# Five blocks of scan output turned by transposing DMAs instead of TensorE, in a hybrid decoder layer

## The chip, the cores and the metric

The kernel runs on one core of a Trainium2 chip. It has five engines with a queue each: TensorE (PE in the profile; its weight loads are PEld), VectorE (DVE), ScalarE (ACT), GpSimd (POOL) and SyncE (SP). The last three also issue DMAs; a DMA that stands in an engine's queue is issued in that queue's order (ACTq, POOLq, SPq). The metric is the device time of one execution in microseconds. The kernel before took 2245.72 us, the median of three runs between 2244.68 and 2250.13.

## The reference

One decoder layer over 2048 tokens of width 1024, with 16 learned meta tokens put in front and dropped at the end. From the normalised input one projection gives everything two branches need. One branch is a state space scan (SSD, Mamba-2) with 16 heads in four groups, behind a short convolution; the other is gated linear attention (GLA) with four heads. Both are normalised, gated and merged:

```python
u = rmsnorm(hres, norm_w)
proj = jnp.einsum('bld,dn->bln', u, w_in)
z, xbc, dt_raw, q, k, v, g_gla, a_lr, merge_g = split_cols(proj, IN_WIDTHS)
xbc = jax.nn.silu(causal_depthwise_conv(xbc, conv_w, conv_b))
...
y = y.reshape(b, l, D_SSD) * jax.nn.silu(z)
y_ssd = rmsnorm(y.reshape(b, l, SSD_GROUPS, D_SSD // SSD_GROUPS), ...)
...
gate_logit = jnp.einsum('blr,rk->blk', a_lr, gla_gate_w2) + gla_gate_b
log_a = jax.nn.log_sigmoid(gate_logit) / GLA_GATE_TEMP
...
y_gla = o.reshape(b, l, GLA_DV) * jax.nn.silu(g_gla)
branches = jnp.stack([y_ssd, y_gla], axis=2)
branch_proj = jnp.einsum('blnc,ncd->blnd', branches, w_branch)
gates = jax.nn.sigmoid(merge_g.reshape(b, l, N_BRANCH, D_MODEL))
merged = jnp.sum(gates * branch_proj, axis=2)
return hres + jnp.einsum('bld,de->ble', merged, w_out)
```

Everything is float32. On TensorE a float32 product is made of three products of operands that are split into a high and a low part.

## The kernel before

The tokens are worked in four blocks of 512; the first block (number 0 in the code) also carries the 16 meta tokens (`m0`). Each block is cut into four chunks of 128 tokens.

The first part of the kernel (to about 1480 us) makes, block by block, the projections and the two scans. A block's projections are a row of *pieces* (`proj_zm`, `proj_conv`, `proj_qk`, `proj_v`, `gla_gates`), and after every piece `step` moves each running side work one step on. The side works are Python generators: `ssd_scan` for each of four groups (started every sixth piece), `gla_scan` for each of four heads, `gates` for the decay of GLA, `fetch_u` for the next block's normalised input. A `yield` in one of them is the border of a step, so a `yield` more puts what follows behind the matmuls of one more piece. TensorE and SyncE keep exactly the order in which the code is written; ScalarE, VectorE and GpSimd are ordered by the tile scheduler, which `tc.issue_after` can bind.

A scan unit (one group or one head of one block) leaves its output as tokens by channels (`yt`, `ot`, 128 tokens x 4 chunks x 256 channels). The second part of the kernel (to the end) needs it as channels by tokens. So every unit ends with eight transposes of 128x128 on TensorE into two PSUM banks (L735 in `ssd_scan`, L974 in `gla_scan`). In `ssd_scan` ScalarE takes them out with the norm weight as scale (L737) into tiles `gg`; in `gla_scan` VectorE multiplies them into the gate tiles `gs`, also named `gg` (L975). Two DMAs on ScalarE's queue store the halves to `y` in memory (L738, L978). GLA units also use a pair of tiles `atp` (a ring of two) for the split attention matrix: ScalarE rounds the high part (L263), VectorE subtracts for the low part (L264), and TensorE multiplies (L214 to L216, in `accum`).

Other places that the change touches: `fetch_u` stores each of the eight tiles of the normalised input (`u_left`, L346) from ScalarE's queue; `load_w` splits weights into a high part on ScalarE (L175) and a low part on GpSimd (L177, tiles `whl`); `gates` makes the decay of the GLA heads in two pairs (products L488 with PSUM banks `pj` and `pt` in the first block, evictions L490 on VectorE and L491 on ScalarE, sums L500); `gla_scan` adds the state of the meta tokens (L881, L882); `make_sums` adds up weights for the second part on GpSimd (L83, stores L86 on ScalarE's queue).

The second part multiplies gates, branches and the output in a scheme of seven products instead of eight (`stages`, sums of weights in `load_a` and `sum_a`). At its end `out_stage` adds the residual (L1250), squares (L1251), takes the root on GpSimd (L1261, L1276), scales (L1283, L1285, L1287) and stores (L1377 on ScalarE's queue, L1432 on SyncE's).

Of the kernel before, what the change touches and what calls it, by code (L numbers as in the profile page):

```python
# [9 lines left out]
F32R = mybir.dt.float32r  # L10
BF16 = mybir.dt.bfloat16
# [4 lines left out]
P = 128  # L16
# [3 lines left out]
BLK = 512  # L20
# [23 lines left out]
def trunk_kernel(ctx: ExitStack, tc: tile.TileContext, xm, xmt, w_feat, w_tok, w_v3, w_zm, w_br, w_o,  # L44
# [225 lines left out]
    def load_u(b):  # L270
# [66 lines left out]
        for kt in range(KT):  # L337
# [8 lines left out]
            nc.scalar.dma_start(u_left[b][kt], xk[:, m0:])  # L346
# [121 lines left out]
    def gates(o):  # L468
# [12 lines left out]
        for h2 in range(0, GH, 2):  # L481
# [14 lines left out]
            for h in (h2, h2 + 1):  # L496
                def sums(h=h):
                    nc.vector.tensor_tensor(gmt[:, h % 2, :tt], gmt[:, h % 2, :tt], g_all[:, h, :tt], op=ALU.subtract)
                    for a, n in chunks:
                        nc.vector.tensor_tensor_scan(g_all[:, h, a:a + n], ones[:, :n], gmt[:, h % 2, a:a + n], 0.0,  # L500
                                                     op0=ALU.mult, op1=ALU.add)
# [81 lines left out]
    def proj_conv(o, g):  # L583
        tt = o.tt
        feats = o.feats[g] = []
        for j in range(4):
# [9 lines left out]
            nc.gpsimd.tensor_copy(tails[:, ti, :], cin[:, tt:tt + 3])  # L596
# [9 lines left out]
    cbs, evicted, convd = {}, [], []  # L606
# [5 lines left out]
    def fetch_cb(o, g, c):  # L612
        cbs[g, c] = cb = mk(spool, [P, 4, P], F32, "cb", bufs=3)
        nc.sync.dma_start(cb, o.cumd[4 * g:4 * g + 4, c * P:(c + 1) * P].unsqueeze(0).to_broadcast([P, 4, P]))

    def ssd_scan(o, g):
# [64 lines left out]
        def after(c):  # L681
# [10 lines left out]
            nc.gpsimd.tensor_tensor(sv, sv, hb(dec[:, ci, hs], P), op=ALU.mult)  # L692
# [36 lines left out]
        yield  # L729
        if not m0 and not g:  # L730
            yield
# [54 lines left out]
    def gla_scan(o, h, last=False):  # L786
# [92 lines left out]
        if m0:  # L879
            ps = bank(pc, "pc")  # L880
# [85 lines left out]
        for c in range(NCH):  # L966
            nc.scalar.activation(ot[:, c], ot[:, c], AF.Identity, scale=r[:, c:c + 1])
        yield
# [256 lines left out]
    def out_stage():  # L1225
        fns, res, ssq, at_once = [], {}, {}, []
# [10 lines left out]
        def use(n, i, t, ps, snap, cols=None):  # L1237
# [13 lines left out]
            nc.scalar.activation(jk[:, c], r[:, c], AF.Square, accum_out=q[:, k:k + 1])  # L1251
            row = n, i, t
            if row == at_once[-1] or (first and (n, i) in [w[:2] for w in at_once[1:]]):
# [4 lines left out]
                if k == 2:  # L1258
                    last = nc.vector.scalar_tensor_tensor(q[:, 0:1], q[:, 2:3], 1.0 / D, q[:, 0:1],
# [5 lines left out]
            elif row in at_once:  # L1265
                scale(*row)
                finish(*row)
# [69 lines left out]
    def load_sum_a(st, n):  # L1337
        st.load_a(n)
        st.sum_a(n)
# [91 lines left out]
    for dst, src in stores:  # L1431
        nc.sync.dma_start(dst, src)  # L1432
# [88 lines left out]
```

## Time and profile before

| | before |
|---|---|
| runs, median (lowest, highest) | 2245.72 us (2244.68, 2250.13) |
| profiled execution | 2246.09 us, span 2244.0 us |
| mean granted TensorE clock | 0.999 |
| TensorE busy | 2213.1 us (99%) |
| VectorE busy | 1574.2 us (70%) |
| ScalarE busy | 1188.8 us (53%) |
| GpSimd busy | 688.1 us (31%) |

Row forms: a timeline row gives start, length, engine, line, operation, output<-input, size, how many were put together, and in brackets how long the engine had been idle and which operation released it. A row of waits gives the engine and line that waited, the engine and line waited for, the total, the number and the longest. A DMA row gives the queue, the number of issues, the size of one and the median time from issue to landing. The chain follows the work back from the last instruction; its rows give start, time on the chain, engine, line. The lines of these rows are lines of the kernel before.

### The profile page before, as it was taken

What the parts mean: (1) busy time and instruction counts of PE and PEld (TensorE: products, weight loads), DVE (VectorE), ACT (ScalarE), POOL (GpSimd) and SP (SyncE); (2) the same over time, 40 slices, a digit from 0 to 9 for tenths busy, and PEclk for the clock granted to TensorE, in tenths of its full rate; (3) what the DMA queues carried; (4) which work ended last, traced back from release to release, by engine and by line L of the source; (5) the groups of instructions that cost most, each with busy time, mean ns of one, the idle gap of its engine ahead of it and who ended that gap; (6) DMA issues with size and microseconds to landing.
All of it is one profiled execution on the core that took longest, in us unless ns stands there. A gap on an engine that the chain in (4) does not pass through costs nothing.

```text
span 2244.0 us, 34943 instructions
## 1 busy us (share of the span) xinstructions
PE 2213.1 (99%) x11789; PEld 1896.7 (85%) x11789; DVE 1574.2 (70%) x2935; ACT 1188.8 (53%) x2767; POOL 688.1 (31%) x681
## 2 busy tenths in 40 slices
PE   7999999999999999999999999999999999999998
PEld 7999999888888888888988888878888888888887
DVE  5786676677657676557577666675678954789876
ACT  5666654476445456545465454454644545454544
POOL 4344433222222122221123100076233374324341
PEclk9999999999999999999999999999999999999999
DMA  8767876767778667778667664386768866677753
GB/s 310 237 226 237 267 257 213 220 207 248 240 250 267 205 215 236 240 250 268 208 219 226 212 216 157 125 260 200 242 220 292 303 221 216 239 281 249 254 178 123
DMA packets 314210, 517.94 MB, mean 231 GB/s; under 512 B 28080, under 2 KB 162480, under 8 KB 314032
## 3 DMA queue, kind: packets, MB, share of 16 engines
q1 hardware_dynamic: 246864, 419.63, 58.1%
q10 hardware_dynamic: 67168, 96.10, 11.8%
q8 instruction: 92, 1.51, 0.3%
q14 instruction: 86, 0.70, 0.1%
HBM read 368.42 MB, written 147.19 MB: 230 GB/s over the span
## 4 chain that ended last, share of the span: by engine, by line
PE 90%; DVE 3%; DMA 3%; ACT 2%; issue 1%; SPq 0%; POOL 0%; POOLq 0%; ACTq 0%; DVEq 0%
PE pj L214 20%; PE pj L216 20%; PE pj L215 20%; PE pt L214 4%; PE pt L215 4%; PE pt L216 4%; PE pc L687 2%; PE pc L214 2%; PE pc L216 2%; PE pc L215 2%; PE pc L848 2%; PE pc L688 1%; PE pc L690 1%; PE pc L956 1%; PE pt L662 1%
## 5 line engine op out<-in xcount | busy, mean ns | idle before, releaser
L214 PE MATMUL pj<-ue,whl 128*128 128x264 f32 (+1 forms) x672 | 236.3, 352 | 3.1 <-ACT g_all L491 2.2
L216 PE MATMUL pj<-ue,whl 128*128 128x264 f32 (+1 forms) x672 | 230.4, 343 | 0.0
L215 PE MATMUL pj<-ue,whl 128*128 128x264 f32 (+1 forms) x672 | 229.5, 342 | 0.0
L214 PE MATMUL pj<-uo,whl 128*128 128x512 f32 x512 | 205.7, 402 | 0.0
L216 PE MATMUL pj<-uo,whl 128*128 128x512 f32 x512 | 200.1, 391 | 0.0
L215 PE MATMUL pj<-uo,whl 128*128 128x512 f32 x512 | 199.4, 389 | 0.0
L215 PE MATMUL pj<-b,a 128*128 128x512 f32 (+1 forms) x484 | 188.0, 388 | 2.2 <-DVE b L1107 2.1
L214 PE MATMUL pj<-b,a 128*128 128x512 f32 (+1 forms) x484 | 188.7, 391 | 0.7 <-DVE io L1250 0.5
L216 PE MATMUL pj<-b,a 128*128 128x512 f32 (+1 forms) x484 | 188.9, 390 | 0.0
L598 DVE SCALAR_TENSOR_TENSOR acc<-cin,hcw,acc 128x512 f32<-128x512 f32 (+1 forms) x192 | 155.5, 810 | 41.6 <-ACT acc L594 40.3
L83 POOL TENSOR_TENSOR wr<-wr 128x256 f32<-128x256 f32 x80 | 67.9, 848 | 375.0 <-DMA wr<-y 160.1
L1132 DVE TENSOR_TENSOR a<-ar,a 128x512 fp32r<-128x512 f32 x160 | 132.8, 837 | 63.3 <-ACT a L1131 60.5
L1122 POOL TENSOR_TENSOR as<-ar,ar 128x512 f32<-128x512 f32 x40 | 63.0, 1575 | 370.3 <-DMA ar<-in_w_br 140.0
L1107 DVE TENSOR_TENSOR b<-br,b 128x512 fp32r<-128x512 f32 x140 | 128.7, 941 | 23.3 <-ACT b L1106 22.4
L214 PEld LDWEIGHTS pj<-ue,whl 128*128 128x128 f32 x672 | 127.0, 189 | 19.4 <-ACT g_all L491 2.4
L216 PEld LDWEIGHTS pj<-ue,whl 128*128 128x128 f32 x672 | 127.1, 189 | 14.9
L215 PEld LDWEIGHTS pj<-ue,whl 128*128 128x128 f32 x672 | 127.1, 189 | 14.7
L177 POOL TENSOR_TENSOR whl<-wr,whl 128x512 fp32r<-128x512 f32 (+1 forms) x76 | 97.8, 1294 | 131.0 <-ACT whl L175 73.6
L1132 DVE TENSOR_TENSOR a<-as,a 128x512 fp32r<-128x512 f32 x120 | 105.7, 882 | 42.5 <-ACT a L1131 39.8
L1166 ACT ACTIVATE sn<-pj 128x512 f32<-128x512 f32 x118 | 69.8, 592 | 122.6 <-PE pj L216 71.7
L1131 ACT ACTIVATE a<-ar 128x512 fp32r<-128x512 f32 x160 | 99.0, 624 | 56.4 <-PE pt L216 24.7
L215 PE MATMUL pt<-b,a 128*128 128x512 f32 x320 | 125.4, 392 | 0.1
(328 smaller groups left out, 6448.4 us busy)
## 6 DMA issues: line engine op xcount, KB each, us to landing
whl<-k_s SPq DMA_DIRECT2D x96, 512.0 KB, 3.7
whl<-k_g SPq DMA_DIRECT2D x96, 512.0 KB, 4.3
whl<-k_v SPq DMA_DIRECT2D x36, 512.0 KB, 4.0
wr<-in_w_feat SPq DMA_DIRECT2D x64, 256.0 KB, 4.5
k_s<-whl SPq DMA_DIRECT2D x32, 512.0 KB, 3.7
cb<-cumd SPq DMA_DIRECT2D x64, 256.0 KB, 5.0
y<-gg ACTq DMA_DIRECT2D x64, 256.0 KB, 4.0
k_g<-whl SPq DMA_DIRECT2D x32, 512.0 KB, 3.9
```

The lines of the kernel that those rows point to most:

```text
L83: nc.gpsimd.tensor_tensor(o, x, y, op=ALU.subtract)
L177: nc.gpsimd.tensor_tensor(hl[:, 1], raw, hl[:, 0].bitcast(F32), op=ALU.subtract)
L214: nc.tensor.matmul(ps, sh, mh, start=first, stop=False, **kw)
L215: nc.tensor.matmul(ps, sh, ml, start=False, stop=False, **kw)
L216: nc.tensor.matmul(ps, sl, mh, start=False, stop=last, **kw)
L598: convd[:] = [nc.vector.scalar_tensor_tensor(acc, cin[:, k:k + tt], hcw[:, ti, k:k + 1], acc, op0=ALU.mult, op1=ALU.add)]
L687: nc.tensor.matmul(py[:, h * 64:(h + 1) * 64], dm[:, h], xdt[:, h], start=True, stop=True)
L1107: nc.vector.tensor_tensor(t[:, 1], raw, t[:, 0].bitcast(F32), op=ALU.subtract)
L1122: nc.gpsimd.tensor_tensor(s1, a21, a22, op=ALU.add)
L1131: nc.scalar.activation(t[:, 0], src, AF.Copy)
L1132: latest[:] = [nc.vector.tensor_tensor(t[:, 1], src, t[:, 0].bitcast(F32), op=ALU.subtract)]
L1166: nc.scalar.activation(sn, self.ps[n, "a"], AF.Copy)
```

## The change

Five units no longer use TensorE for the turn: the last SSD group (g = 3) of the second, third and fourth block, and the second GLA head (h = 1) of the second and third. A new helper, `turn_by_dma`, copies the unit's float32 values as 16-bit words into two `atp` tiles, one with the low and one with the high half-words (two ScalarE copies, L625), transposes each with a transposing DMA on ScalarE's queue (L627, back into `yt` or `ot`), waits one step (two for SSD), and lets GpSimd put the half-words together again (four copies, L635) in the `atp` tiles. For SSD the scaling then runs on ScalarE one step later (L758) and the stores another step later (L761); for GLA VectorE multiplies from the `atp` tiles (L1004) and the store follows a step later (L1007).

With it come six smaller edits: the u stores of the first block go from ScalarE's to GpSimd's queue; `gates` has a step more between its two pairs in the first block; the product of the GLA meta state takes a `pt` bank instead of a `pc` bank; the sums of weights of the second part are called apart from their loads, three products later for the first 28; the scaling of the row before the last is put behind the last square; and the last two stores change places, the very last on ScalarE's queue.

ScalarE at the SSD unit g = 3 of the second block, before. L737 are the two evictions with scale, L738 the stores of y, `tok_1217` is the unit's output:

```order
L810 ACTIVATE act_7663<-g_all_5230 128x512
L307 ACTIVATE acc_7793,ss_1308_7726<-acc_7793 128x512
L749 ACTIVATE act_7675<-pj_7676 128x512
L737 ACTIVATE gg_7711<-pt_7706,hsw 128x512
L737 ACTIVATE gg_7719<-pt_7714,hsw 128x512
L738 DMA y_1_6_110<-gg_7711 128x512
L738 DMA y_1_7_111<-gg_7719 128x512
L263 ACTIVATE kdt_7735<-pt_7730 128x512
L852 ACTIVATE c_1297_7666<-pc_7747 128x256
```

The same engine and place now. First the two copies and the transposes:

```order
L843 ACTIVATE act_7663<-g_all_5230 128x512
L625 ACTIVATE atp_7706<-tok_1217_7293 128x1024
L625 ACTIVATE atp_7707<-tok_1217_7293 128x1024
L308 ACTIVATE acc_7783,ss_1306_7716<-acc_7783 128x512
L782 ACTIVATE act_7675<-pj_7676 128x512
L627 DMA_TRANSPOSE tok_1217_7293<-atp_7706 128x8x128
L627 DMA_TRANSPOSE tok_1217_7293<-atp_7707 128x8x128
L264 ACTIVATE kdt_7725<-pt_7720 128x512
L885 ACTIVATE c_1297_7666<-pc_7737 128x256
```

And ten rows on, the scaling and the stores, with the split of the next GLA unit's attention (`atp_7954`) behind them:

```order
L87 DMA gate_t_1_161<-wr_7851 256x1x256
L87 DMA gate_t_1_165<-wr_7852 256x1x256
L778 ACTIVATE act_7895<-pj_7896 128x512
L758 ACTIVATE atp_7706<-atp_7706,hsw 128x512
L758 ACTIVATE atp_7707<-atp_7707,hsw 128x512
L761 DMA y_1_6_110<-atp_7706 128x512
L761 DMA y_1_7_111<-atp_7707 128x512
L869 ACTIVATE sq_8101<-sq_8101 128x4x64
L870 ACTIVATE sq_8101<-sq_8101 128x4x64
L264 ACTIVATE atp_7954<-sq_7951 128x2x128
```

The scaling and the stores moved down past ten rows, and the next writer of an `atp` tile now follows the stores that read the ring's tiles; the stores of `gate_t` moved down as well.

VectorE at the second GLA head of the second block, before; L975 are the multiplications that take the turned output from PSUM:

```order
L906 TENSOR_TENSOR sq_8852<-act_7901,act_7962 128x512
L855 COPY_PREDICATED c_1485_8571<-msk,pc_8742 128x256
L264 TENSOR_TENSOR tok_1506_8666<-pj_8667,tok_1505_8665 128x512
L975 SCALAR_TENSOR_TENSOR gg_7788<-pt_8816,hgw,gg_7788 128x512
L264 TENSOR_TENSOR tok_1506_8666<-pj_8668,tok_1505_8665 128x512
L975 SCALAR_TENSOR_TENSOR gg_7854<-pt_8822,hgw,gg_7854 128x512
L855 COPY_PREDICATED c_1485_8571<-msk,pc_8828 128x256
L264 TENSOR_TENSOR sq_8859<-sq_8852,sq_8858 128x512
L855 COPY_PREDICATED c_1485_8571<-msk,pc_8840 128x256
L855 COPY_PREDICATED c_1485_8571<-msk,pc_8900 128x256
L782 SCALAR_TENSOR_TENSOR gg_8891<-gg_8891,pj_8862 128x512
```

And now; L1004 are the multiplications, which take it from the `atp` tiles that GpSimd joined:

```order
L939 TENSOR_TENSOR sq_8850<-act_7895,act_7958 128x512
L888 COPY_PREDICATED c_1483_8569<-msk,pc_8746 128x256
L265 TENSOR_TENSOR tok_1504_8664<-pj_8665,tok_1503_8663 128x512
L888 COPY_PREDICATED c_1483_8569<-msk,pc_8826 128x256
L265 TENSOR_TENSOR sq_8857<-sq_8850,sq_8856 128x512
L265 TENSOR_TENSOR tok_1504_8664<-pj_8666,tok_1503_8663 128x512
L888 COPY_PREDICATED c_1483_8569<-msk,pc_8838 128x256
L1004 SCALAR_TENSOR_TENSOR gg_7778<-atp_8728,hgw,gg_7778 128x512
L888 COPY_PREDICATED c_1483_8569<-msk,pc_8898 128x256
L1004 SCALAR_TENSOR_TENSOR gg_7844<-atp_8729,hgw,gg_7844 128x512
L815 SCALAR_TENSOR_TENSOR gg_8889<-gg_8889,pj_8860 128x512
```

The multiplications moved down four rows, the second one behind the last select (`COPY_PREDICATED`) of that level.

TensorE at the second pair of gate products of the first block, before; they (L488) follow the conv products of bank `pj_1357` and precede the scan step (L662 on):

```order
L215 MATMUL pj_1357<-ue_369,whl_1389 128x264
L216 MATMUL pj_1357<-ue_369,whl_1389 128x264
L488 MATMUL pj_1435<-act_1005,w_387 128x264
L488 MATMUL pt_1439<-act_1005,w_387 128x264
L488 MATMUL pj_1443<-act_1005,w_387 128x264
L488 MATMUL pt_1447<-act_1005,w_387 128x264
L662 MATMUL pt_1455<-cst,act_682 128x128
```

And now (L489 is the same product):

```order
L216 MATMUL pj_1471<-ue_369,whl_1504 128x264
L217 MATMUL pj_1471<-ue_369,whl_1504 128x264
L215 MATMUL pj_1472<-ue_369,whl_1504 128x264
L216 MATMUL pj_1472<-ue_369,whl_1504 128x264
L217 MATMUL pj_1472<-ue_369,whl_1504 128x264
L489 MATMUL pj_1550<-act_1005,w_387 128x264
L489 MATMUL pt_1554<-act_1005,w_387 128x264
L489 MATMUL pj_1558<-act_1005,w_387 128x264
L489 MATMUL pt_1562<-act_1005,w_387 128x264
L686 MATMUL pt_1568<-cst,act_682 128x128
```

The four products moved down past a scan step and the 48 products of the next conv piece (banks `pj_1471`, `pj_1472`).

The diff, without the three one-line bindings (`pooled`) that keep GpSimd's joining copies behind the last GpSimd work named there:

```diff
-            nc.scalar.dma_start(u_left[b][kt], xk[:, m0:])
+            (nc.gpsimd if m0 else nc.scalar).dma_start(u_left[b][kt], xk[:, m0:])
...
                 yield
+            if m0 and not h2:
+                yield
...
+    def turn_by_dma(src, more=True):
+        flat = src.rearrange("p c f -> p (c f)").bitcast(U16)
+        words = flat.rearrange("p (n w) -> p n w", w=2)
+        back = flat.rearrange("p (w k t) -> p w k t", w=2, t=P)
+        tiles = [mk(wk, [P, BLK], F32, "atp", bufs=2) for _ in range(2)]
+        for w in range(2):
+            nc.scalar.activation(tiles[w].bitcast(U16), words[:, :, w], AF.Copy)
+        for w in range(2):
+            nc.scalar.dma_start_transpose(back[:, w], tiles[w].bitcast(U16))
+        yield
+        if more:
+            yield
+        with tc.issue_after(pooled[-1].ins):
+            for j in range(2):
+                dst = tiles[j].bitcast(U16).rearrange("p (c t w) -> p c t w", w=2, t=P)
+                for w in range(2):
+                    nc.gpsimd.tensor_copy(dst[:, :, :, w], back[:, w].rearrange("p (c j) t -> p c j t", j=2)[:, :, j])
+        if more:
+            yield
+        return tiles
...
+        if not m0 and g == 3:
+            tiles = yield from turn_by_dma(yt)
+            for j in range(2):
+                with behind():
+                    nc.scalar.activation(tiles[j], tiles[j], AF.Identity, scale=hsw[:, 2 * g + j:2 * g + j + 1])
+            yield
+            for j in range(2):
+                nc.scalar.dma_start(y_left[0][o.b][2 * g + j], tiles[j])
+            return
...
-            ps = bank(pc, "pc")
+            ps = bank(pt, "pt")
             nc.tensor.matmul(ps[:, :256], btm[:META], s_gla[:META, h], start=True, stop=True)
...
+        if not m0 and o.b < nblk - 1 and h == 1:
+            tiles = yield from turn_by_dma(ot, False)
+            for j, t in enumerate(tiles):
+                nc.vector.scalar_tensor_tensor(gs[j], t, hgw[:, j:j + 1], gs[j], op0=ALU.mult, op1=ALU.mult)
+            yield
+            for j in range(2):
+                nc.scalar.dma_start(y_left[1][o.b][2 * h + j], gs[j])
+            return
...
                 if k == 2:
+                    with tc.issue_after(squared.ins):
+                        finish(*unfinished.pop())
...
                 scale(*row)
-                finish(*row)
+                if row == at_once[-2]:
+                    unfinished.append(row)
+                else:
+                    finish(*row)
...
-            at(i - LOAD + (n % 2), lambda st=st, n=n: load_sum_a(st, n))
+            pos = i - LOAD + (n % 2)
+            at(pos, lambda st=st, n=n: st.load_a(n))
+            at(pos + (3 if i < 28 else 0), lambda st=st, n=n: st.sum_a(n))
...
-    for dst, src in stores:
-        nc.sync.dma_start(dst, src)
+    early, late = stores[-2:]
+    for (dst, src), q in zip(stores[:-2] + [late, early], [nc.sync] * (len(stores) - 1) + [nc.scalar]):
+        q.dma_start(dst, src)
```

More of the change, by code (lines that the diff above doesn't have):

```diff
@@ L10 @@
 F32R = mybir.dt.float32r
+U16 = mybir.dt.uint16
 BF16 = mybir.dt.bfloat16
@@ L595, in proj_conv @@
                                                    bias=hcb[:, ti:ti + 1])]
-            nc.gpsimd.tensor_copy(tails[:, ti, :], cin[:, tt:tt + 3])
+            pooled[:] = [nc.gpsimd.tensor_copy(tails[:, ti, :], cin[:, tt:tt + 3])]
             for k in range(3):
@@ L604, in proj_conv @@
             yield
-    cbs, evicted, convd = {}, [], []
+    cbs, evicted, convd, pooled = {}, [], [], []
     def behind():
@@ L691, in after @@
             sv = s_ssd[:, g].rearrange("p (h c) -> p h c", c=64)
-            nc.gpsimd.tensor_tensor(sv, sv, hb(dec[:, ci, hs], P), op=ALU.mult)
+            pooled[:] = [nc.gpsimd.tensor_tensor(sv, sv, hb(dec[:, ci, hs], P), op=ALU.mult)]
             nc.vector.tensor_tensor(s_ssd[:, g], s_ssd[:, g], pst[:, :256], op=ALU.add)
@@ L1225, in out_stage @@
     def out_stage():
-        fns, res, ssq, at_once = [], {}, {}, []
+        fns, res, ssq, at_once, unfinished = [], {}, {}, [], []
         def fetch(n, i, t):
```

5 lines of the change are left out of this document (1 added, 4 removed).

## The prediction, made before the changed kernel ran

> **What bounds the kernel now.** I read the page first: the busy time by engine and the shares of the chain of waits.
> ```profile
> span 2244.0 us, 34943 instructions
> PE 2213.1 (99%) x11789; PEld 1896.7 (85%) x11789; DVE 1574.2 (70%) x2935; ACT 1188.8 (53%) x2767; POOL 688.1 (31%) x681
> PE 90%; DVE 3%; DMA 3%; ACT 2%; issue 1%; SPq 0%; POOL 0%; POOLq 0%; ACTq 0%; DVEq 0%
> ```
> TensorE is busy 99% of the span and makes up 90% of the chain, so time goes only where TensorE gets less work, where one of its few waits shrinks, or behind its last matmul; anything that makes it wait adds directly. Next I read what TensorE waits for.
> ```profile
> PE pj L214 <- ACT g_all L491: 2.2, 1, 2.2
> PE pc L848 <- DVE s_gla L882: 0.8, 1, 0.8
> PE pj L488 <- ACT acc L594: 0.6, 1, 0.6
> ```
> The columns are total wait, number of waits, longest. These three lie in places that the change edits.
>
> **Part one, the transposes that leave TensorE.** Five units lose eight transposes each: the last SSD group in the second, third and fourth block, and the second GLA head in the second and third. Two of the three SSD units and one of the GLA units stand in the chain like this (start, time on the chain):
> ```profile
> 632.25 0.88 PE pt L735 x8
> ...
> 731.02 0.87 PE pt L974 x8
> ...
> 938.64 0.87 PE pt L735 x8
> ```
> Each eight hold TensorE's chain for 0.87 us, with matmuls close on both sides. All of it is on the path: 5 x 0.87 = **-4.35 us**.
>
> What takes their place is a longer road. ScalarE copies out two sets of half-words (128x1024 each), two transposing DMAs run on its queue, GpSimd puts the halves together in four copies, and then the scaling and the store follow. The trace has no transposing DMA and no such GpSimd copy; the nearest rows are these (the two DMA rows: size, median from issue to landing).
> ```profile
> 105.74 1.07 ACT L493 ACTIVATE g_all<-g_all 128x1056 f32<-128x1056 f32 x1
> 633.70 0.90 ACTq L738 DMA_DIRECT2D y<-gg  x2
> y<-gg ACTq DMA_DIRECT2D x64, 256.0 KB, 4.0
> ar<-m SPq DMA_DIRECT2D x32, 256.0 KB, 5.7
> L83 POOL TENSOR_TENSOR wr<-wr 128x256 f32<-128x256 f32 x80 | 67.9, 848 | 375.0 <-DMA wr<-y 160.1
> 99.06 0.41 POOL L596 COPY tails<-cin 128x3 f32<-128x3 f32 x1
> ```
> A half-word copy of 128x1024 costs about 1.07 us on ScalarE, which is 53% busy. The pair of transposes moves 2 x 256 KB: 4.0 us if the two run side by side like the y stores, 11.4 us (2 x 5.7) if one follows the other at the slowest of these landings. A GpSimd copy of 128x512 lies between 0.41 (hardly any data) and some 1.7 us (twice the 848 ns of half its elements); I take 1.0, so four are 4 us. From the ScalarE copies to the joined tile that is 2.1 + 4.0 + 4 = 10 us at best and 17.5 at worst by these rows.
>
> **What waits for it, GLA head.** In the second block ScalarE's rows L967 and VectorE's and TensorE's rows around it are:
> ```profile
> 725.40 0.90 ACT L967 ACTIVATE ot<-ot,rstd 128x256 f32<-128x256 f32 x2
> 727.29 0.63 ACT L263 ACTIVATE sq<-sq 128x512 fp32r<-128x512 f32 x1 [0.99 <-DVE sq L906]
> ...
> 738.73 0.44 DVE L855 COPY_PREDICATED c<-msk,pc 128x256 f32<-128x256 uint8 x1 [3.94 <-PE pc L848]
> 739.06 0.68 DVE L782 SCALAR_TENSOR_TENSOR gg<-gg,pj 128x512 f32<-128x512 f32 x1
> ...
> 741.35 0.73 DVE L928 COPY_PREDICATED sq<-msk,pt 128x512 f32<-128x512 uint8 x1
> ...
> 744.87 0.22 PE pt L935 x2
> ```
> The scaling ends at 726.3; two copies (2.1) and the 0.63 split that stands behind them put the transposes' issue near 729.2. VectorE's multiplications of the joined tiles stand on both sides of the 738.73 row, and ahead of the L928 select that TensorE's L935 products at 744.87 need. From the second multiplication (0.6, like the 739.06 row less its overlap) to the end of L928 (739.06 to 742.08, 3.0) VectorE has 3.6 us of work, so it may start at 741.2 without TensorE feeling it. With 4 us of GpSimd copies the transposes may land at 737.2: 8 us after their issue. Between 4.0 and 11.4 I take the side of the y stores, since these go from the same queue in the same pair: the head costs nothing, hidden under VectorE's 3.94 us of waiting. Beyond 8 us each microsecond costs two, one per block. Queued behind a late multiplication on VectorE are the selects and the next unit's level products.
>
> **What waits for it, SSD group.** Here the scaling stands two steps later on ScalarE, and the store behind it reads the joined tile itself. That tile comes from a ring of two which the next GLA unit writes too. ScalarE and TensorE there, before:
> ```profile
> 652.24 0.60 ACT L745 ACTIVATE act<-pj 128x512 f32<-128x512 f32 x1 [5.29 <-PE pj L216]
> 655.73 0.40 ACT L263 ACTIVATE atp<-sq 128x256 fp32r<-128x256 f32 x1
> 664.93 0.42 DVE L264 TENSOR_TENSOR atp<-pt,atp 128x256 fp32r<-128x256 f32 x1
> 666.19 0.47 PE L214 MATMUL pc<-tok,atp 128*128 128x256 f32 x1
> ...
> 666.97 0.47 PE L214 MATMUL pc<-tok,atp 128*128 128x256 f32 x1
> ```
> The two half-word copies take the place of the 633.70 stores and end near 635.7; with 4 to 8 us of transposes and 4 us of GpSimd's copies the joined tile is there by 648. The scaling comes near 652.9, the stores leave at about 655, and the split of 655.73 must now wait until they have landed: 655 + 4.0 = 659, 3.3 us later. TensorE reads that tile at 666.2, but VectorE's and ScalarE's later splits of the unit slide with it (the 664.93 one ends at 665.35, TensorE wants it at 666.97). Bounds: 0 if the slack holds all of it, 3.3 a block if nothing does. I take 0.5 a block, since 1.6 us of slack at the last split covers half of the slide and both engines idle in between: **+1.5 us** for three blocks.
>
> **Part two, the gate products of the first block.** A step is added between the two pairs of heads, so the second pair's four products move behind the next scan step and 48 conv products. Before:
> ```profile
> 97.85 0.39 PE L488 MATMUL pj<-act,w 48*128 48x264 f32 x1 [0.62 <-ACT acc L594]
> 97.86 3.98 DVE L500 TENSOR_TENSOR_SCAN g_all<-ones_r,tok 128x16 f32<-128x16 f32 x5
> 102.59 0.48 ACT L491 ACTIVATE g_all<-pj,pv 128x264 f32<-128x264 f32 x1 [3.54 <-DVE tok L490]
> 103.13 0.39 PE L214 MATMUL pj<-ue,whl 128*128 128x264 f32 x1 [2.16 <-ACT g_all L491]
> 105.43 0.42 PE L214 MATMUL pj<-ue,whl 128*128 128x264 f32 x1
> 100.00:120.00 20.00, 17.06 (x123) 16.49 (x122) 16.75 (x33) 15.83 (x36) 5.55 (x7) 0.91 0.50 156
> ```
> VectorE's prefix sums hold up the eviction of the gate products, TensorE waits 2.16 + 0.62 us, and after the wait its matmuls run at a pitch of 0.22 instead of 0.12 us for some 3 us (the clock of this stretch, first number behind the brackets, is 0.91): some 1.5 us more. Together 4.3 us hang on this place. The products go on using the two banks that the conv products rotate through, though: counted forward at 0.12 us a product, TensorE reaches the third gate product at about 105.0, while the conv bank it needs is evicted only after VectorE's accumulations, near 108.4 by my count. That gap of about 3.4 us replaces the old one. Ends: -4.3 (it closes wholly) and +1 (the new one is longer); I take **-0.8**, near the difference of the gaps.
> The moved GLA product of the meta tokens no longer shares a bank with L848, so the 0.8 us wait on s_gla L882 quoted above goes: between -0.8 and 0 (another transpose of that bank late instead), taken **-0.8**.
>
> **Part three, u stores of the first block on GpSimd's queue.** Eight stores move from ScalarE's queue (0.33 us each there) to stand between GpSimd's weight subtractions; as GpSimd is in order, a late store holds the next subtraction and the weights of the next projection.
> ```profile
> 15.45 0.35 ACTq L346 DMA_DIRECT2D u<-act  x1
> 21.27 1.33 POOL L177 TENSOR_TENSOR whl<-wr,whl 128x288 fp32r<-128x288 f32 x1 [7.38 <-DMA wr<-in_w_zm]
> 25.25 1.35 POOL L177 TENSOR_TENSOR whl<-wr,whl 128x288 fp32r<-128x288 f32 x1 [0.49 <-ACT whl L175]
> ```
> Five of them fall into the 7.38 us in which GpSimd idles anyway. The other three stand singly. At a price between 0.33 (ScalarE's queue) and 1.3 us (a subtraction) the one before the 25.25 row moves it by up to 0.5 us. Ends 0 and +1.3, taken **+0.5** from a price of 1.0, nearer GpSimd's own rows than ScalarE's.
>
> **Part four, the end.** After TensorE's last product:
> ```profile
> 2236.92 0.42 DVE L1250 SCALAR_TENSOR_TENSOR io<-pj,io 128x256 f32<-128x256 f32 x1 [0.26 <-PE pj L216]
> 2237.07 0.72 ACT L1283 ACTIVATE io<-io,ssf 128x512 f32<-128x512 f32 x1 [1.18 <-POOL ssf L1276]
> 2237.70 0.40 ACT L1251 ACTIVATE junk<-io 128x256 bf16<-128x256 f32 x1
> 2239.91 0.82 SPq L1432 DMA_DIRECT2D out_h<-io  x2
> ```
> The last square waits behind the scaling of the row before (2237.07); now it goes first and could start at 2237.34, when its input is ready: -0.36, say -0.34. The last two stores were issued one after another by SyncE in 0.82 us; now the last goes from ScalarE at once: -0.41. Together **-0.75**; the ends are 0 and -0.75.
> The split of the weight sums in the later half (three products later in the first 28) leaves GpSimd's rows and their waits in the same order, so it does nothing.
>
> **The sum.** -4.35 - 0.75 - 0.8 - 0.8 + 0.5 + 1.5 = -4.7 us on the profiled execution's 2246.09 (span 2244.0): 2241.4. The median of the runs, 2245.72, is 0.37 lower, which gives **2241.0**.
>
> **The rivals.**
> First, the transposes are slow (ends slower). At 11.4 us from issue to landing the GLA head costs 2 x (11.4 - 8) = 6.8 us. An SSD unit's copies, scaling and stores slide by 3 to 4 us on top of the 3.3, hardly any of which is covered: with 1.6 us of slack, about 3 more a block, 9 in all. 2241 + 6.8 + 9 - 1.5 = about 2255. It decides from about 10 us up. For it speaks that no row here moves half-words and that a plain 256 KB already took 5.7; against it, that the bytes are the same as in the y stores' 4.0.
> [...]
> Second, the tile ring holds ScalarE and VectorE fully: 3.3 us x 3 = 9.9 instead of 1.5, 2249.4. For it, that the split must wait for a store to land; against it, 10 us between 655.73 and TensorE's use at 666.19.
> Third, the gap in the gates closes: -4.3 instead of -0.8, 2237.5. For it, that the prefix sums no longer hold the eviction; against it, the bank count above.
> Fourth, the edits at the gates, the bank and the end change nothing on the path: 2245.7 - 4.35 + 1.5 + 0.5 = 2243.4. For it, that each of the three is worth less than 1 us by the sum; against it, that the end's rows leave nothing to hide behind.
>
> **How the numbers follow.** My own case has 0.52 with the fourth beside it (2239 to 2245); slow transposes 0.16, a held ring 0.14, the closed gap 0.18. A measurement of this kernel tells about 0.3% from no change: below 2239.0 is faster, above 2252.5 slower. Faster is the third rival, 0.18; slower is the first and a third of the second (which may reach 13 us with any lateness of the transposes), 0.21; the rest, 0.61, is the same. The range runs from the closed gap less 1 us, 2236.5, to the held ring with a small stall of the GLA head, 2252; what lies above is the slow transposes.
>
> **What would show it.** Right: the transposes' landing at 4 to 8 us, no wait of TensorE in 640 to 1340 us, TensorE with 40 fewer transposes, the gap at 103 us moved to about 105. Wrong: TensorE waits on products whose releaser is VectorE after L1004, or on atp after L761; VectorE idle behind a GpSimd copy L635; weight loads late because GpSimd's in-order rows and the gate stores behind them wait for a transpose.

## The result, and the profile after

The changed kernel takes 2250.03 us (median of 22 runs, 2246.06 to 2256.60); the kernel before took 2246.84 us beside it (22 runs, 2244.68 to 2251.68). The ratio is 1.0013, 95% interval 1.0008 to 1.0019: slower by some 3 us, where 2241.0 and a gain of 4.7 us had been forecast. The profiled execution has a span of 2250.0 us against 2244.0.

The page of the changed kernel, span and busy time, the DMA packets of both kernels (first the one before, then the changed one), and the groups of the new DMA issues (count, median from issue to landing):

```profile
span 2250.0 us, 34937 instructions
PE 2210.5 (98%) x11749; PEld 1893.5 (84%) x11749; DVE 1573.6 (70%) x2935; ACT 1197.1 (53%) x2777; POOL 706.4 (31%) x709
```
```profile
DMA packets 314210, 517.94 MB, mean 231 GB/s; under 512 B 28080, under 2 KB 162480, under 8 KB 314032
```
```profile
DMA packets 324259, 520.57 MB, mean 231 GB/s; under 512 B 38640, under 2 KB 173040, under 8 KB 324080
tok<-atp ACTq DMA_TRANSPOSE x6, 8.5
ot<-atp ACTq DMA_TRANSPOSE x4, 5.5
```

TensorE has the 40 matmuls less and 2.6 us less busy time, and the span is longer all the same. The ten transposing DMAs add 10,560 packets of less than 512 bytes (1,056 each), and one of them lands after 8.5 us in the SSD units and after 5.5 in the GLA heads, in the median.

TensorE's waits in the changed kernel (total, number, longest):

```profile
PE pt L216 <- DVE b L1148: 3.9, 3, 1.7
PE pj L489 <- ACT acc L597: 3.1, 1, 3.1
PE pj L215 <- DMA whl<-k_g: 2.7, 1, 2.7
PE pc L215 <- DVE c L977: 2.1, 4, 0.7
PE pj L215 <- DVE gg L815: 1.3, 2, 0.9
PE pt L968 <- DVE sq L961: 1.1, 1, 1.1
```

New are the wait for a weight load (2.7 us) and those on L815 and L961, which stand behind the GLA heads' turn. TensorE's wait at the gate products was 2.2 us for ScalarE's L491; now its L489 waits 3.1 us for ScalarE's L597. The first row is the start of the second part, where the traces of all kernels differ by up to 2 us.

Where the time goes is seen best by laying the two traces side by side: how much later the same TensorE instruction starts than in the trace of before (worked out from the starts of matched matmuls; negative is earlier). The change between two rows is what the stretch between them cost. The last three columns are kernels of the experiments below.

| at (us, time of before) | changed | changed, again | no turns | plain copies | GLA ring freed |
|---|---|---|---|---|---|
| 60 | -0.08 | -2.31 | -1.26 | -0.48 | -1.47 |
| 140 (behind the gates) | -1.73 | -3.11 | -3.25 | -1.43 | -2.09 |
| 440 (behind the first block) | -3.27 | -4.88 | -5.08 | -3.26 | -3.92 |
| 625 | -2.69 | -4.88 | -5.08 | -3.26 | -3.92 |
| 660 (behind the second block's SSD unit) | +2.89 | -1.53 | -4.72 | -2.81 | -0.71 |
| 728 | +3.65 | +0.21 | -4.16 | -2.20 | +0.14 |
| 760 (behind its GLA head) | +3.48 | +0.02 | -4.16 | -3.08 | -0.74 |
| 975 | +4.07 | +0.84 | -3.16 | -2.64 | 0.00 |
| 990 (behind the third block's SSD unit) | +3.19 | -0.03 | -3.16 | -3.52 | -0.76 |
| 1075 | +3.65 | +0.46 | -2.59 | -3.90 | -0.84 |
| 1110 (behind its GLA head) | +5.25 | +1.96 | -2.59 | -4.68 | -0.61 |
| 1325 | +5.74 | +3.05 | -2.75 | -3.65 | +0.49 |
| 1345 (behind the fourth block's SSD unit) | +4.87 | +2.18 | -2.75 | -4.52 | -0.38 |
| 2236 | +6.18 | +2.20 | -2.81 | -3.23 | +2.50 |

The changed kernel is ahead by 3 to 5 us when the first turn by DMA comes. It then loses 5.6 us at the SSD unit of the second block (3.4 us in a second profile of the same program), and the two GLA heads cost 1.4 us together instead of saving 1.7. The SSD units of the third and fourth block save the 0.87 us each that was forecast.

The second block's SSD unit in the changed kernel, from the timelines of ScalarE's queue, SyncE's queue, GpSimd and TensorE:

```profile
631.55 1.38 ACTq L627 DMA_TRANSPOSE tok<-atp  x1
632.97 2.29 ACTq L627 DMA_TRANSPOSE tok<-atp  x1
```
```profile
633.79 7.41 SPq L172 DMA_DIRECT2D whl<-k_g  x2
```
```profile
640.94 0.77 POOL L635 COPY atp<-tok 128x512 uint16<-128x512 uint16 x1 [7.38 <-DMA tok<-atp]
...
646.23 2.10 POOL L635 COPY atp<-tok 128x512 uint16<-128x512 uint16 x3 [3.87 <-DMA tok<-atp]
```
```profile
646.47 0.80 PE L215 MATMUL pj<-uo,whl 128*128 128x512 f32 x1 [2.73 <-DMA whl<-k_g]
647.06 0.63 PE L216 MATMUL pj<-uo,whl 128*128 128x512 f32 x1
...
652.87 0.39 PE L215 MATMUL pj<-uo,whl 128*128 128x512 f32 x1
```

and its chain of waits (start, time on the chain), with the stretches by window (the first number behind the brackets is TensorE's granted clock):

```profile
633.79 12.63 DMA whl<-k_g
```
```profile
635.00:645.00 10.00, 8.73 (x47) 7.34 (x45) 4.53 (x13) 4.09 (x10) 1.42 (x2) 1.00 1.13 134
645.00:655.00 10.00, 8.53 (x25) 6.77 (x26) 2.19 (x6) 1.21 (x3) 4.94 (x7) 0.66 0.68 242
655.00:665.00 10.00, 10.00 (x57) 8.65 (x56) 7.26 (x14) 4.82 (x12) 3.33 (x4) 1.00 0.97 314
```

GpSimd's rows tell the landings: the first transpose at 640.8, the second at 646.2, some 14.6 us after the first was issued and 13.2 after its own issue. A weight load `whl<-k_g` that SyncE issued at 633.79 takes 12.63 us; the median of such loads was 4.3 in the kernel before. TensorE waits 2.73 us for it and then gets a clock of 0.66 over ten microseconds: a matmul takes 0.63 instead of 0.39. The wait and the slow stretch are the 5.6 us (2.7 and some 3.2, less the 0.3 that the traces show saved at 631 us). By stretches of half a microsecond the granted clock is 0.50 from 645.8 to 652.7 us, for 6.8 us, and 1.00 before and behind it; this is called the half clock below. Behind TensorE's wait of 3.12 us at the gate products it lasted 3.4 us (109.9 to 113.3 us), as it did behind that of 2.16 us in the kernel before (104.5 to 108.0 us). What sets its length is not shown.

The GLA head in the second block, changed kernel, VectorE and ScalarE with its queue:

```profile
739.64 1.13 DVE L1004 SCALAR_TENSOR_TENSOR gg<-atp,hgw,gg 128x512 f32<-128x512 f32 x1 [1.70 <-POOL atp L635]
...
743.92 0.69 DVE L815 SCALAR_TENSOR_TENSOR gg<-gg,pj 128x512 f32<-128x512 f32 x1 [1.35 <-ACT gg L814]
```
```profile
740.80 0.35 ACTq L1007 DMA_DIRECT2D y<-gg  x1
743.29 0.60 ACT L814 ACTIVATE gg<-pj 128x512 f32<-128x512 f32 x1 [7.47 <-DMA y<-gg]
```

The first multiplication waits 1.70 us for GpSimd, as the prediction feared. What follows it is worse: the eviction L814 of the next gate tile waits until the store of 740.80 has landed, since it writes into the ring of four `gg` tiles from which that store reads. VectorE's L815 and then its select L961 come later by that, and TensorE waits on both (1.3 us and 1.1 us over the two heads, in its rows above).

### The profile page after: what moved, and what is told of

Its sections match the earlier page's. It is cut to its first block, busy times and chain, and to the rows that moved or that the text cites. A ratio compares the mean times of both kernels' runs of the same rounds, so it can differ in the third digit from the quotient of the medians.

```text
span 2250.0 us, 34937 instructions
## 1 busy us (share of the span) xinstructions
PE 2210.5 (98%) x11749; PEld 1893.5 (84%) x11749; DVE 1573.6 (70%) x2935; ACT 1197.1 (53%) x2777; POOL 706.4 (31%) x709
## 4 chain that ended last, share of the span: by engine, by line
PE 66%; DMA 3%; DVE 3%; ACT 2%; issue 1%; POOL 1%; ACTq 0%; SPq 0%; POOLq 0%; DVEq 0%
PE pj L215 14%; PE pj L217 14%; PE pj L216 14%; PE pt L216 4%; PE pt L215 4%; PE pt L217 4%; PE pc L215 2%; PE pc L217 2%; PE pc L216 2%; PE pc L711 1%; DMA acc<-in_xmt 1%; PE pc L712 1%; PE pc L714 1%; PE pc L881 1%; PE pc L989 1%
## 5 line engine op out<-in xcount | busy, mean ns | idle before, releaser
L1163 POOL TENSOR_TENSOR as<-ar,ar 128x512 f32<-128x512 f32 x40 | 58.8, 1470 | 382.3 <-DMA ar<-in_w_br 166.1
```

Source lines behind the costliest of these rows:

```text
L1163: nc.gpsimd.tensor_tensor(s1, a21, a22, op=ALU.add)
```

## Experiments: which part loses

Four kernels, each timed beside the kernel before. First all five units go back to TensorE; the small edits stay.

```diff
-        if not m0 and g == 3:
+        if False:
...
-        if not m0 and o.b < nblk - 1 and h == 1:
+        if False:
```

> The changed kernel with all five units turned by TensorE as before; the other edits stay. Theory (the turns by DMA lose, above all at the SSD unit of the second block, where the transposes crowd a weight load, TensorE waits 2.7 us and then runs 6.8 us at half clock): 2 to 4 us below the kernel before, that is 2243 to 2245 beside 2246.8, with no wait on a weight load near 645 us. Rival (the small edits at the gates, the bank and the end lose what the turns gain): at or above the kernel before.

Measured: 2243.32 us beside 2246.21, ratio 0.9988 (0.9980 to 0.9997). The small edits gain 2.7 us by the ratio; the turns lose this and some 3 us more. No wait for a weight load.

The converse, the kernel before with the five turns alone (all edits outside `turn_by_dma` and its two callers undone):

> The kernel before with the five turns by DMA alone (the split of the weight sums stays, which changes no order). Theory (the turns lose): 4 to 7 us above the kernel before, about 2252, with the wait near 645 us. Rival (the turns gain, the small edits lose): 2 to 4 us below it.

Measured: 2257.39 us, ratio 1.0054 (1.0039 to 1.0068), 11 to 12 us above before and more than either theory said. Its GLA head in the second block shows the largest part, 3.9 us between 728 and 760 us by the starts of matched matmuls, in the rows of ScalarE and its queue, and in a row of TensorE's waits:

```profile
742.18 0.36 ACTq L1005 DMA_DIRECT2D y<-gg  x1
748.18 0.60 ACT L812 ACTIVATE gg<-pj 128x512 f32<-128x512 f32 x1 [11.46 <-DMA y<-gg]
```
```profile
PE pt L966 <- DVE sq L959: 5.5, 3, 3.3
```

Here the store took some 6 us to land instead of 2.4, the eviction came that much later, and TensorE waited 3.3 us, with a clock of 0.91 over the 20 us around it. The place is the same as in the changed kernel, with more of it. Why this store took so long is not shown.

The SSD units alone by DMA (the first edit left out, the second kept), and the GLA heads alone:

> The changed kernel with the two GLA heads turned by TensorE, the three SSD units by DMA. Theory (the loss sits at the SSD unit of the second block): as the changed kernel, 2249 to 2251, and TensorE waits for the weight load near 645 us. Rival (the GLA heads hold VectorE, which waited 4.2 us for the joined tiles in the changed kernel): 2246 or less.

> The changed kernel with the three SSD units turned by TensorE, the two GLA heads by DMA. Theory (the loss sits at the SSD unit of the second block): 2244 to 2246, near the kernel without any turn by DMA. Rival (the GLA heads hold VectorE): 2248 or more.

Measured: SSD units alone 2243.43 us, ratio 0.9987 (0.9978 to 0.9995); GLA heads alone 2244.90, ratio 0.9994 (0.9985 to 1.0002), as the theory had it. The expectation for the SSD units failed: this kernel does not lose, and its profile has no wait near 645 us. Its load behind the transposes landed after 9.3 us, just in time. The two parts together lose more than the sum of the two (0.1 and 1.6 us above the kernel without turns, each known to some 2 us), which no theory had foreseen; so the changed kernel was run again beside other kernels.

## Experiments: the second block's SSD unit

> The changed kernel itself, on the chip of this call. The kernels without the GLA turns and without the SSD turns were both faster than before, the kernel with all of them slower, though the first two share its program up to 730 us and 620 us. If the loss is the program's own: 2249 to 2251 beside 2246. If it hung on the chip of the first comparison: 2244 to 2246, the sum of the single turns' effects (0.1 and 1.6 us on 2243.3).

Measured: 2247.79 us beside 2245.74, ratio 1.0016 (1.0005 to 1.0027), so the loss comes with the program, though the time lies between the two that were expected. The same wait stands in its profile, somewhat shorter, with a half clock of 3.4 us behind it:

```profile
PE pj L215 <- DMA whl<-k_g: 1.8, 1, 1.8
```

The changed kernel with that one unit back on TensorE:

```diff
-        if not m0 and g == 3:
+        if o.b > 1 and g == 3:
```

> The changed kernel with the SSD unit of the second block turned by TensorE, the four other units by DMA. Theory (that unit's transposes crowd the weight load that TensorE waits for near 645 us): 4 to 6 us below the changed kernel of the same call, no wait for a weight load near 645 us. Rival (the loss is spread over all turns or lies in the GLA heads): within 1.5 us of the changed kernel.

Measured: 2247.02 us, ratio 1.0007 (0.9998 to 1.0016). The wait for the load is gone, but only 0.8 us are gained, not 4 to 6: in this profile the GLA heads cost 1.6 and 2.2 us (728 to 760 and 1075 to 1110 us) where the changed kernel's cost -0.2 and 1.6. By its number the rival holds (within 1.5 us of the changed kernel); the wait is real, but the loss is not at one place.

One SSD unit, in the second block, as the only turn; and the kernel before with the two copies and the two transposing DMAs made for nobody:

```diff
+            for w in range(2):
+                nc.scalar.activation(tiles[w].bitcast(mybir.dt.uint16), words[:, :, w], AF.Copy)
+            for w in range(2):
+                nc.scalar.dma_start_transpose(back[:, w], tiles[w].bitcast(mybir.dt.uint16))
```

> The kernel without turns by DMA, and only the SSD unit of the second block turned by DMA. Theory: the weight load issued just behind the transposes lands 9 to 13 us after its issue instead of 4.3, and TensorE waits for it if that is over some 10 us; all other places as without turns. Rival (it takes several turns): the load lands as before, no wait.

> The kernel before, and at the SSD unit of the second block the two half-word copies and the two transposing DMAs are made as well, with nobody reading their result (TensorE still turns the unit, no joining copies on GpSimd). Theory (the DMAs alone crowd the load): the weight load behind them lands 8 us or more after its issue. Rival (the chain over GpSimd, the gate stores and SyncE delays it): it lands in 4 to 5 us as in the kernel before.

Measured, one execution each: 2240.92 us with the one turn, 2245.71 us with the idle transposes. In the first the load lands after 9.1 us, in the second after 8.0, and nobody waits for it. The second settles which road the delay takes: neither GpSimd nor a store hangs on these transposes, and the load is late all the same. In every trace with a turn here the load lands within 0.3 us of the second transpose, though it was issued 0.6 to 0.8 us behind it on another queue. By kernel, from the traces (the pair from the first issue to the last landing):

| kernel | pair lands (us) | load lands (us) | TensorE waits (us) |
|---|---|---|---|
| changed | 14.6 | 12.6 | 2.7 |
| changed, again | 14.1 | 11.7 | 1.8 |
| GLA ring freed | 13.8 | 11.7 | 1.8 |
| turns only | 13.9 | 11.4 | 1.5 |
| SSD turns, again | 13.1 | 10.7 | 0.3 |
| second block's SSD and third block's GLA | 12.5 | 10.5 | 0.6 |
| SSD turns | 11.7 | 9.3 | 0 |
| one SSD turn | 11.5 | 9.1 | 0 |
| idle transposes | 10.7 | 8.0 | 0 |

In these rows the delay costs nothing below a load time of some 10 us (9.3 us: no wait); above it TensorE waits for what is over (12.6 us: 2.7). From 1.8 us of waiting on the half clock came as well in these rows (6.8 us of it in the first row, 3.4 us in the second and third); at another place two waits of 1.72 us passed without it (ending at 1486 and 1490 us in the changed kernel, granted clock 1.00 from 1484 to 1500 us).

A second pair of transposes ahead of the first, of the same tiles into unused `gg` tiles, on the kernel with one SSD turn:

> The kernel with one SSD unit of the second block turned by DMA, with a second pair of transposing DMAs of the same tiles into unused gate tiles ahead of it. Theory (the transposes hold the DMA engines): the weight load issued behind them lands 14 to 20 us after its issue (one pair: 9 to 13, none: 4.3) and TensorE waits 4 to 9 us for it, with the half clock after it. Rival: the load lands as with one pair.

Measured: 2246.07 us in one execution. The expectation failed. The pairs landed after 5.9 and 10.7 us, the two loads after 8.2 and 9.0 us, and TensorE did not wait for them. SyncE held another load (`acc`) back until 635.85 us, by the profile because it waited 4.3 us for the first of the added transposes, so the weight loads came only when the first pair was about to land. The kernel does not measure the double crowd it was made for.

## Experiments: the transposes themselves, and the ring

Plain DMAs of the same bytes, on the same queue, in place of the transposing ones. The joining copies and all waits stay; the output of the five units is left unturned:

```diff
-            nc.scalar.dma_start_transpose(back[:, w], tiles[w].bitcast(U16))
+            nc.scalar.dma_start(back[:, w].rearrange("p k t -> p (k t)"), tiles[w].bitcast(U16))
```

> The changed kernel with plain DMAs of the same bytes on the same queue in place of the transposing ones; the five units stay unturned, so this kernel leaves the turn out. Theory (the transposing DMAs themselves crowd the weight loads and land late): the copies land in 2 to 4 us, the weight load near 645 us lands in 4 to 6 us after its issue and nobody waits for it; 3 to 5 us below the changed kernel, 2243 to 2245. Rival (the longer road over ScalarE and GpSimd costs it, whatever the DMA): as the changed kernel.

Measured: 2242.11 us beside 2246.65, ratio 0.9979 (0.9969 to 0.9988): 4.5 us faster than before, and by the ratios some 8 us faster than the changed kernel, more than the theory's 3 to 5. The DMA issues around the second block's SSD unit (629 to 652 us), first with transposing DMAs (the changed kernel), then with plain ones:

```profile
whl<-k_g SPq DMA_DIRECT2D x5, 512.0 KB, 6.7
tok<-atp ACTq DMA_TRANSPOSE x2, 11.2
```
```profile
whl<-k_g SPq DMA_DIRECT2D x5, 512.0 KB, 4.0
tok<-atp ACTq DMA_DIRECT2D x2, 256.0 KB, 4.2
```

The copies land after 4.2 us, the loads beside them after 4.0, and all turns but the one of the second block's SSD unit save their 0.87 us (table above). So the longer road over ScalarE and GpSimd costs nothing at these four places; the transposing DMAs do. Their late landing and their longer hold of ScalarE's queue (1.3 to 2.3 us for each issue, against 0.5 to 0.6) are not parted by this run.

The ring: VectorE multiplies into the joined tiles, and the store leaves from there.

```diff
-                nc.vector.scalar_tensor_tensor(gs[j], t, hgw[:, j:j + 1], gs[j], op0=ALU.mult, op1=ALU.mult)
+                nc.vector.scalar_tensor_tensor(t, t, hgw[:, j:j + 1], gs[j], op0=ALU.mult, op1=ALU.mult)
...
-                nc.scalar.dma_start(y_left[1][o.b][2 * h + j], gs[j])
+                nc.scalar.dma_start(y_left[1][o.b][2 * h + j], tiles[j])
```

> The changed kernel, and at the two GLA heads VectorE multiplies into the joined tiles and the stores leave from there, so that the gate tiles (ring of four) come free with the multiplication and not with the landing of the store. Theory (ScalarE's next eviction L814 waits for that landing, which holds VectorE's L815 and TensorE): L814 comes some 2 us earlier, 1 to 2 us gained at each of the two heads, 2 to 4 in all beside the changed kernel. Rival (VectorE's wait for the joined tiles alone is the cost): no gain.

Measured: 2245.01 us, ratio 0.9993 (0.9984 to 1.0003), beside 1.0016 and 1.0013 of the changed kernel in other comparisons: some 5 us by the ratios, known to some 2 us; the traces show 2 us of it at the two heads. The eviction now follows the store at once:

```profile
737.95 0.35 ACTq L1007 DMA_DIRECT2D y<-atp  x1
738.34 0.60 ACT L814 ACTIVATE gg<-pj 128x512 f32<-128x512 f32 x1 [6.05 <-PE pt L953]
```

In the traces the head of the second block then saves 0.88 us (728 to 760 us), that of the third costs 0.2 instead of 1.5 to 1.6. TensorE's wait for the load near 645 us is still there, 1.8 us. The joined tiles stand in a ring too: ScalarE waits 2.77 us there for the landing of the store (at 741.71 us), but TensorE reads the tile that is written next only at 751.5 us, and in this profile it did not wait.

The same kernel with the second block's SSD unit back on TensorE:

> The previous kernel with the SSD unit of the second block turned by TensorE: two SSD units and two GLA heads by DMA. Theory: 1 to 3 us below the kernel without any turn by DMA, 2240 to 2243. Rival (each turn by DMA costs what it saves): 2243 to 2246.

Measured: 2243.63 us, ratio 0.9988 (0.9979 to 0.9996). In its profile all four turns save 0.7 to 0.9 us, and still it ends level with the kernel without any turn (0.9988), as the rival had it. It gives back 1.3 us between 1110 and 1140 us, 1.3 between 1470 and 1510 and 1.2 later; which of that the turns owe is not shown, for the kernel without turns loses 1.2 us at another place (760 to 900 us).

## Experiments: what stayed open

> The SSD unit of the second block and the GLA head of the third block turned by DMA, the three others by TensorE. If a later GLA turn changes the early unit: its pair of transposes lands 13 us or more after its issue and TensorE waits for the weight load, as in the changed kernel. If it was chance: 10 to 14 us, as likely without a wait.

> The kernel with the three SSD units turned by DMA once more. If the later turns matter: the pair of the second block lands after 10.5 to 12 us, no wait for the weight load, 2 to 3 us below the kernel before again. If it was chance: 11 to 15 us, and a wait of 1 to 3 us with the half clock is as likely.

> Only the SSD units of the third and fourth block turned by DMA. Theory (these two save 0.87 us each and cost nothing, as the alignment of the traces shows at 981 and 1331 us): 1.5 to 2 us below the kernel with no turn by DMA, 4 to 5 us below the kernel before. Rival: within 0.7 us of the kernel with no turn by DMA.

Measured: 2246.78 us, ratio 1.0000 (0.9990 to 1.0009), for the second block's SSD unit with the third block's GLA head; 2243.05 us, ratio 0.9990 (0.9981 to 0.9999), for the SSD turns again; 2244.62 us, ratio 0.9990 (0.9982 to 0.9999), for the SSD units of the third and fourth block alone. In the first two the second block's pair landed after 12.5 and 13.1 us and TensorE waited 0.6 and 0.3 us:

```profile
PE pj L215 <- DMA whl<-k_g: 0.6, 1, 0.6
```
```profile
PE pj L215 <- DMA whl<-k_g: 0.3, 1, 0.3
```

So the SSD turns alone reach the edge as well: the same program gave 11.7 us once and 13.1 the next time. That later GLA turns lengthen the pair is not shown; chance within 10.7 to 14.6 us could give the rows. It is not excluded either: the four longest pairs of the table are those of the four traces with all five turns. The third kernel fell short of its expectation of 4 to 5 us: its profile has the two gains at 981 and 1331 us, but the third block's pair landed after 13.2 us this time (6.9 to 10.3 elsewhere) and 1.7 us were lost behind it by 1050 us. What makes the landing vary by several microseconds between executions stays open. A profile is one execution: those of the freed ring (2248.20 us) and of the repeated SSD turns (2246.08) were 3 us slower than the medians of these kernels, that of the third kernel here (2241.08) 3.5 us faster, so what a trace loses is not what a typical run loses.

The kernels that turn every unit and beat both the kernel before and the changed one are the one without turns by DMA (0.9988), the one with the SSD turns alone (0.9987, 0.9990), the one with the SSD turns of the third and fourth block (0.9990) and the freed ring without the second block's unit (0.9988). They can't be told apart; turning by DMA is worth nothing measurable here.

## Why the prediction was wrong

The step that failed is the one that chose the landing time of the transposes: "between 4.0 and 11.4 I take the side of the y stores". They land like nothing in the trace of before: pairs of 6.8 to 14.6 us in the changed kernel. With it failed the silent assumption that only what reads the transposed words waits for them: a load on another queue waited too. The first rival had the right mechanism in its outline, 11.4 us and a loss, but with a chance of 0.16, and it put the cost at the wrong places. With DMAs that land as the step assumed, the kernel takes 2242.1 us, 1.1 us from the forecast. That closeness is partly luck: the small edits gained 2.7 us instead of 1.85, and the turns by plain copies 2.0 instead of 2.85, so two errors cancel. That 2250.0 lies below the upper end of 2252 is luck too: this end was set by a tile ring that holds ScalarE and VectorE, and TensorE lost nothing by that ring.

- The transposes that leave TensorE (-4.35): held at four of the five places, each of which steps by 0.76 to 0.88 us in the traces. At the second block's SSD unit they show between a gain of 0.5 and a loss of 0.5 before the wait for the load begins. There not all of it was on the path: with TensorE's eight transposes gone, its next ones (L902) wait for VectorE's L839, by 0.16 to 1.08 us in nine of the ten traces that have this turn, against 0.13 us at most where TensorE still makes it.
- The wait at the SSD turns (+1.5, thought to come from the ring of `atp` tiles): the ring held ScalarE's split, as said (2.42 us for the landing of the store, at 661.1 us), and TensorE lost nothing by it. What cost 3 to 6 us in the changed kernel's profiles was not in the sum: a weight load on another queue that lands with the transposes, 12.6 and 11.7 us after its issue in the two profiles. The prediction named late weight loads among the signs of being wrong, but by the chain over GpSimd's rows and the stores; the idle transposes show that it needs no such chain.
- The GLA heads (0): the pair landed after 6.8 and 7.8 us in the changed kernel, just within the 8 us that the prediction allowed, and most of GpSimd's copies took 0.77 us instead of 1.0; VectorE did wait 1.7 to 2.2 us for the joined tiles. But the bound was reckoned from VectorE's work alone. The store of the product, later by a step, keeps a `gg` tile that ScalarE's next eviction needs; freeing it gave back some 2.1 us at the two heads. That ring was not looked at, though the prediction had reckoned just this for the `atp` ring.
- The gates (-0.8): the count of banks was right, the third product came at 104.9 and 108.5 us with a wait of 3.12 (forecast: 105.0, 108.4 and 3.4). With the half clock behind it counted in, the place is worth 0.4 to 2.0 us by trace (94 to 140 us): 2.0 in the three traces where the half clock lasted 3.4 us, as before, and 0.4 to 1.0 where it lasted 6.8.

```profile
104.87 0.39 PE L489 MATMUL pj<-act,w 48*128 48x264 f32 x1
105.09 0.28 PE L489 MATMUL pt<-act,w 48*128 48x264 f32 x1
108.50 0.39 PE L489 MATMUL pj<-act,w 48*128 48x264 f32 x1 [3.12 <-ACT acc L597]
```

- The meta state's bank (-0.8): 1.5 to 1.8 us between 270 and 440 us in all kernels that have the edit: 1.08 at 420 us, where the wait on the list stood, and 0.14 at each of three other such products; most of the rest, some 0.3 at 308 us, comes without the edit too.
- The u stores (+0.5): no loss seen; one takes 0.54 us on GpSimd, not 1.0, and by 60 us the kernels with the edit are 0.1 to 2.7 us ahead, against 0.8 ahead and 0.5 behind in two kernels without it, which says only that it doesn't hurt.
- The end (-0.75): about -0.1. The last stores were issued earlier, as forecast, but landed later: the last one, from ScalarE's queue with two of SyncE's in flight, took 3.04 us, where it had taken 2.26 behind its neighbour on one queue (both from the traces). From TensorE's last matmul to the span's end it is 7.26 us after 7.36.

```profile
2243.62 0.42 ACT L1292 ACTIVATE junk<-io 128x256 bf16<-128x256 f32 x1 [1.55 <-DVE io L1291]
...
2245.09 0.72 ACT L1329 ACTIVATE io<-io,ssf 128x512 f32<-128x512 f32 x1 [0.35 <-POOL ssf L1304]
...
2245.84 0.34 ACTq L1477 DMA_DIRECT2D out_h<-io  x1
```

- The sums of weights: that the edit does nothing was read from the order and not run by itself.

Taken together the small edits bring 2.7 us (ratio 0.9988; the sum had 1.85), and the turns lose some 6 us (from 0.9988 to 1.0013 and 1.0016; the sum had a gain of 2.85).

## What to carry to other kernels

A DMA that takes work from the busiest engine must be priced by what else is in flight: here a pair of transposes delayed the load behind it on another queue until its own landing (8.0 to 12.6 us after its issue, against a median of 4.3 before), and each load time above the slack of some 10 us was paid by TensorE, with a clock of 0.50 for 3.4 to 6.8 us on top behind the three longest waits (1.8 to 2.7 us). When a step's result is stored later, follow every ring whose tile that store reads to its next writer. Replace a doubtful operation by a plain one of the same size, with all waits kept: that one run separated the transposes from the road around them.

## What the runs showed of the hardware that was not expected

A transposing DMA of 128x1024 half-words landed after 3.2 us at best and 13.2 at worst in the changed kernel, a plain DMA of the same bytes at the same places after 2.4 to 4.9. It held ScalarE's queue for 1.3 to 2.3 us at its issue, the plain one for 0.5 to 0.6, and made 1,056 packets under 512 bytes. A wait of TensorE of 2.73 us cost more than itself, by the half clock that came with it (0.50 for 6.8 us, 0.66 over ten microseconds).
